# Merging the mixers of a two-layer backbone: rows transposed and routed before their norm is known, and where the last layer's first expert weights are split

## The chip, the cores and the metric

One core of one Trainium2 chip. The metric is the device time of one launch in microseconds (us); the median of three runs of the kernel before is 2865.58 us. The engines are named as the profile names them: PE multiplies matrices (PEld loads its weights), DVE is the vector engine, ACT the scalar engine, POOL GpSimd; SP issues most transfers.

## What is computed

Two layers of a backbone over 1024 latent tokens of 1024 features and 256 context tokens (layer 0 alone carries the context on). Each layer mixes tokens in four groups, merges them into the stream with one projection, and sends the stream through 16 experts that each choose their tokens. The part that matters here, from the reference:

```python
def _modulate(x, g, shift, scale):
    return _rmsnorm(x, g) * (1 + scale) + shift
...
xl = xl + gt1 * mix_l
xl = xl + gt2 * _ec_moe(_modulate(xl, norm2_g[i], sh2, sc2), router_w[i], ...)
...
def _ec_moe(h, router_w, w_gate, w_up, w_down):
    aff = softmax((h @ router_w).astype(float32), axis=-1)
    cap = max(1, EC_CAPACITY_FACTOR * N // N_EXPERTS)
    gates, idx = top_k(swapaxes(aff, 1, 2), cap)
    xs = h[idx]
```

With r a row's reciprocal norm, a2 = g (1 + scale) and b2 = shift, a row that the experts see is h = r (x a2) + b2, and its 16 logits are r ((x a2) W) + b2 W. Each expert takes the 128 tokens of largest probability.

## The kernel before, in words

A layer runs in stages: norm, projections, the mixers (a software pipeline over heads), `merge`, `moe`. In `merge` PE multiplies the mixers' outputs with the output projection, a tile of 128 tokens at a time, in two halves m of 512 columns. Both factors are in two parts of 12 bits, so a product takes three matmuls (`mm3`), and a half is 8 steps k of three: 24 matmuls into the PSUM tile `mixp`. Layer 0 has ten tiles (eight of tokens, two of context), layer 1 eight.

Everything else of the stage is put between these matmuls by hand. `Line` is a list of generators; after each step k `line.tick()` runs what is due, and a `yield n` puts the next piece n ticks later. Inside `manual_schedule` PE, DVE and ACT execute in the order in which the program records, so the ticks set where a piece stands in each engine's queue. An engine whose next instruction waits holds up everything behind it. The generators are:

- `residual` (L1274 to L1334), one for each half: the products times the gate (L1281), the residual added (L1282), a sum of squares on ACT. After the second half come the reciprocal norm (`rstd_steps`, with a power on POOL and four corrections on DVE), the norm and the modulation in two halves (L1306 on DVE, L1308 on POOL, on DVE for the last pair), the row's way to DRAM (`hrow`), and two groups of four transposes (`h2p`) with their copies into `h2T`.
- `router`, after each second tile, for two tiles: 8 matmuls on four column groups of PE (`lg`), a copy (`lpart`), 2 matmuls that add the groups (`lgs`), and a softmax on DVE and ACT. POOL splits the probabilities for the later gathers (`take`).
- `prep`, for each pair of tiles: the four groups' norms, transposes (`cTp`) and two parts of the left factors of the next pair (L1228 on ACT, L1230 on DVE).
- `vectors`: the modulation's vectors on all partitions (a2 is made at L1250); for the context once more.
- `best_four`, `best_six`, `best_all` and, in layer 0, `best_ctx`: lists of the largest probabilities, sorted and joined by chains of short DVE instructions (L1392 to L1430), then the slot of each token (`assign`, L1462 to L1493). `best_all` ends with `columns(0)`: DVE marks the slots of an expert (`hot`, L1507), PE turns them into row numbers (`tkp`), DVE writes these as integers (`tkii`, L1519).

`moe` starts with an indirect DMA that POOL issues: it gathers the first expert's rows from `hrow` into `xg` (L1552). PE transposes them (`pT`), ACT and DVE split them (`xs`), and the products with the experts' weights begin (`moeP`). The weights come as pages of 1 MB (`ewr`), of which every 128 rows are a step: ACT writes the upper part (`ewh`), DVE the lower one (`ewl`, L107). The first steps have their lower part made on POOL: 12 in layer 1, of which 8 stand ahead of the gather in POOL's queue and 4 behind it; 4 in layer 0, 1 ahead and 3 behind. While layer 0's merge ends, PE also multiplies the next layer's modulation (`ada_p`).

```python
AHEAD, BEHIND = (4, 12), (3, 4)
...
stream = weights()
ready = [next(stream) for _ in range(AHEAD[i] - BEHIND[i])]
xg0 = gather_tokens(self.first[0])
ready += [next(stream) for _ in range(BEHIND[i])]
```

Of the kernel before, what the change touches and what calls it, by code (L numbers as in the profile page):

```python
# [14 lines left out]
ALU = mybir.AluOpType  # L15
# [29 lines left out]
# rows of the small vectors, per layer  # L45
# [8 lines left out]
class Line:  # L54
    """work in steps beside a main stream; a step yields the number of ticks to the next one (1 without)"""
# [23 lines left out]
class Kernel:  # L79
# [48 lines left out]
    def rstd_steps(self, out, ss, n, width, pool=False):  # L128
        """out = 1 / sqrt(ss / width + eps), n columns; pool: without the scalar engine's tables"""
# [26 lines left out]
    def setup(self):  # L156
# [8 lines left out]
        # small vectors, one feature per partition  # L165
# [6 lines left out]
        # silu of the two conditioning vectors, padded to 32 columns  # L172
# [6 lines left out]
    def tables(self):  # L179
        """constants, side by side in one array"""  # L180
# [21 lines left out]
        # tokens of the same tile that come before  # L202
# [36 lines left out]
    def mod_feature(self, i, m):  # L239
        """the first norm's scale and shift, one feature per partition: modA, modB [128, 2 (c, ctx), 8 k]"""  # L240
# [4 lines left out]
        # chunk j, slice s -> feature (4j + s) of 16: vector j // 2, k = 4 (j % 2) + s  # L245
# [9 lines left out]
    def mod_row(self, out, i, v, c):  # L255
        """vector v of the six of layer i on all partitions: out [128, 1024]"""
# [7 lines left out]
    def take_x(self, t):  # L264
        """a token tile of x; of the rows loaded before the last expert's output was there, with it added"""
# [15 lines left out]
    def normed(self, t0, n):  # L281
        """x * rstd of token tiles"""
# [12 lines left out]
    def normed_T(self, xn, k):  # L295
        """128 features of the tiles, transposed"""
# [5 lines left out]
    def norm1_start(self):  # L302
        """the first tiles without the modulation"""
# [11 lines left out]
    def norm1(self, i, side, start, then):  # L315
        """then: called after the first group of tiles"""
# [23 lines left out]
    def h(self, part, k, t0, n):  # L340
        """hT columns of n tokens from t0 (t0 >= 1024: context)"""
# [7 lines left out]
    def proj_latent(self, i):  # L349
        """token-major qc | kvc | kr (416 columns)"""  # L350
# [28 lines left out]
    def proj_va(self, i):  # L379
        """values of group A, token-major, [hi | lo] side by side: [128 tokens, 2 tiles, head, 2, 64]"""  # L380
# [27 lines left out]
    def proj_feat(self, i, c0, put, putc):  # L408
        """feature-major 256 columns from c0: put and putc (latent, context) take features 128 m .. and the first token"""
# [29 lines left out]
    def put_q(self, tiles, alloc):  # L439
        """queries of group A, scaled: head h as [hi; lo] on the halves of the partitions (odd heads [lo; hi])"""  # L440
# [10 lines left out]
    def put_k(self, tiles, alloc):  # L451
        """keys of group A: head h as [hi; hi] and [lo; lo]"""
# [15 lines left out]
    def pool_buf(self, n):  # L468
        """[128, n + 16] with zeros around the n tokens"""
# [18 lines left out]
    def pool_mix(self, w, us, n, out):  # L488
        """us: two pool_bufs of 128 features; out(t, p): takes the 256 outputs of token tile t"""
# [5 lines left out]
        for m, u in enumerate(us):  # L495
            # position 8 + t holds token t; window sums of the lower and the upper 64 features
# [28 lines left out]
    def fno_weights(self, i):  # L525
        """[cos part | sin part] of the channel transform times fno_w: [128, 2 k, 512]"""
# [37 lines left out]
        # fold t with N - t: cosine sums see X[t] + X[N - t], sine sums X[t] - X[N - t]  # L564
# [56 lines left out]
    def fourier_ctx(self, i, fl, out):  # L621
        """fl [128, 2, 256]"""
# [28 lines left out]
    def untranspose(self, cT, n, out):  # L651
        """two of [128, n * 128] feature-major to token-major"""
# [11 lines left out]
    def pt_steps(self, hi, lo, P, nchunk):  # L664
        """transposes of P [128 q, nchunk * 128] into hi, lo: [128 keys, chunk, 128 q] views"""
# [1383 lines left out]
```

## Time and profile before

| | |
|---|---|
| three runs | 2858.80, 2865.58, 2865.62 us; median 2865.58 |
| the profiled execution's own time: its span, first to last instruction | 2861.3 us, 4.3 below the median |
| PE, share of the span | 94% |
| DVE, ACT, POOL | 73%, 60%, 14% |
| merge of layer 0, first to last `mixp` | 593.8 to 733.2 us |
| from there to the first expert product | to 777.66 us |
| merge of layer 1 | 2084.7 to 2193.2 us |
| from there to the first expert products without a gap | to 2256.96 us |

No time outside the span is recorded for the profiled execution, so the span stands for its time. The page divides time by engine, by source line and into 40 slices; the chain of waits goes back from the last instruction to what released each one. A row of the timeline has the start, the duration, the engine, the line, the operation with output and inputs, and in brackets how long the engine was idle and who ended that. Rows of the same kind in a row are put together (x3), and their duration is that of all of them. Rows of matmuls overlap, so the cost of one is the distance between starts.

### The profile page before, as it was taken

The numbers are of one execution on the slowest core, as the hardware profiler recorded it, in microseconds if no ns is written. First come the engines' busy times: TensorE is split into PE (matmuls) and PEld (weight loads), VectorE is DVE, ScalarE is ACT, GpSimd is POOL, SyncE is SP. The second block draws the span as 40 slices with busy tenths as digits, with TensorE's granted clock in tenths as the row PEclk, the third lists the DMA queues.
The fourth block names the chain that finished last, engine by engine and source line by source line (L and its number), as shares of the span: only waits on it lengthen the run. The fifth ranks groups of instructions, "written<-read, shape, count | busy, mean of one in ns | idle before, by whom it ended". The sixth has DMA issues, their size and how long they took to land. (4 is left out here: it accounts for less than half of the span.)

```text
span 2861.3 us, 46062 instructions
## 1 busy us (share of the span) xinstructions
PE 2688.6 (94%) x16912; PEld 2130.0 (74%) x16912; DVE 2096.3 (73%) x4289; ACT 1704.0 (60%) x3272; POOL 401.1 (14%) x436
## 2 busy tenths in 40 slices
PE   7999899999699999999999999999997599999996
PEld 5788788887377677677676788888885488888874
DVE  5624687867877777777766842687868899899997
ACT  5422687964255555555544631598953477777774
POOL 0000120222301010101100000120223311000112
PEclk9999999999799999999999999999998799999998
DMA  7642301145578787887778554201154699999996
GB/s 302 216 140 63 92 22 49 56 160 206 215 283 293 271 295 276 281 283 284 282 281 292 162 200 135 60 24 56 57 184 152 245 360 380 359 387 387 383 385 224
DMA packets 228106, 628.22 MB, mean 220 GB/s; under 512 B 32390, under 2 KB 87302, under 8 KB 227880
## 3 DMA queue, kind: packets, MB, share of 16 engines
q1 hardware_dynamic: 206088, 578.54, 55.2%
q0 software_dynamic: 21648, 46.67, 6.5%
q8 instruction: 134, 2.20, 0.3%
q14 instruction: 92, 0.75, 0.1%
q10 hardware_dynamic: 144, 0.07, 0.0%
HBM read 564.20 MB, written 61.01 MB: 219 GB/s over the span
## 5 line engine op out<-in xcount | busy, mean ns | idle before, releaser
L106 ACT ACTIVATE ewh<-ewr 128x1024 fp32r<-128x1024 f32 x768 | 765.6, 1055 | 312.8 <-DMA ewr<-exp_w_down 97.6
L107 DVE TENSOR_TENSOR ewl<-ewr,ewh 128x1024 fp32r<-128x1024 f32 x752 | 873.5, 1217 | 74.6 <-ACT ewh L106 73.1
L113 PE MATMUL moeP<-ewh,xs 128*128 128x512 f32 x2048 | 670.1, 401 | 6.6 <-DVE xs L107 6.6
L113 PEld LDWEIGHTS moeP<-ewh,xs 128*128 128x128 f32 x2048 | 387.9, 190 | 107.1 <-issue 11.2
L113 PE MATMUL moeP<-ewl,xs 128*128 128x512 f32 x1024 | 407.1, 398 | 0.0
L113 PE MATMUL moeP<-ewh,ehs 128*128 128x512 f32 x1024 | 331.8, 397 | 1.7 <-ACT ewh L106 1.5
L113 PEld LDWEIGHTS moeP<-ewh,ehs 128*128 128x128 f32 x1024 | 192.2, 188 | 58.6 <-issue 12.3
L113 PEld LDWEIGHTS moeP<-ewl,xs 128*128 128x128 f32 x1024 | 194.5, 190 | 40.7
L113 PE MATMUL moeP<-ewl,ehs 128*128 128x512 f32 x512 | 201.7, 394 | 0.0
L113 PE MATMUL mixp<-woh,cT 128*128 128x512 f32 x576 | 201.6, 407 | 0.0
L1602 PE MATMUL cx<-ewr,cxo 128*32 128x256 f32 x3072 | 186.3, 382 | 0.0
L107 DVE TENSOR_TENSOR ptl<-pT,pth 128x512 fp32r<-128x512 f32 (+2 forms) x288 | 164.2, 580 | 19.4 <-ACT pth L106 18.4
L122 PE MATMUL pT<-ident,PA 128*128 128x128 f32 x928 | 145.7, 275 | 8.3 <-ACT oh L714 3.7
L1602 PEld LDWEIGHTS cx<-ewr,cxo 128*32 128x32 f32 x3072 | 90.1, 109 | 84.5 <-issue 34.6
L106 ACT ACTIVATE pth<-pT 128x512 fp32r<-128x512 f32 (+2 forms) x288 | 149.6, 536 | 4.3 <-PE pT L122 1.3
L1653 POOL DMA_INDIRECT xacc<-ey,tkii x31 | 49.3, 1589 | 703.4 <-PE cx L1602 472.7
L1103 DVE TENSOR_REDUCE mxA<-SD 128x1 f32<-128x512 f32 (+1 forms) x192 | 114.5, 597 | 38.5 <-PE SD L113 37.8
L122 PEld LDWEIGHTS pT<-ident,PA 128*128 128x128 f32 x928 | 112.5, 141 | 32.5 <-ACT oh L714 5.8
L113 PEld LDWEIGHTS mixp<-woh,cT 128*128 128x128 f32 x576 | 108.2, 188 | 25.3 <-issue 3.5
L113 PE MATMUL SD<-kT,qT 96*128 96x512 f32 x384 | 119.9, 420 | 5.7 <-ACT PA L1117 5.3
L113 PE MATMUL mixp<-wol,cT 128*128 128x512 f32 x288 | 113.3, 393 | 0.0
L1552 POOL DMA_INDIRECT xg<-hrow,tkii x32 | 57.0, 1782 | 400.5 <-ACT ehs L106 97.6
(413 smaller groups left out, 5266.4 us busy)
## 6 DMA issues: line engine op xcount, KB each, us to landing
ewr<-exp_w_gate SPq DMA_DIRECT2D x128, 1024.0 KB
ewr<-exp_w_up SPq DMA_DIRECT2D x128, 1024.0 KB
ewr<-exp_w_down SPq DMA_DIRECT2D x128, 1024.0 KB
ada_w<-ada_w SPq DMA_DIRECT2D x96, 512.0 KB
qkv<-qkvr SPq DMA_DIRECT2D x18, 512.0 KB
xacc<-xm SPq DMA_DIRECT2D x18, 512.0 KB
hrow<-xm SPq DMA_DIRECT2D x18, 512.0 KB
x<-xacc SPq DMA_DIRECT2D x18, 512.0 KB
```

The lines of the kernel that those rows point to most:

```text
L106: self.nc.scalar.activation(hi, src, AF.Copy)
L107: (lo_on or self.nc.vector).tensor_tensor(lo, src, f32(hi), ALU.subtract)
L113: self.nc.tensor.matmul(out, l, r, start=start, stop=stop)
L122: self.nc.tensor.transpose(out, src, self.ident[:p, :p])
L1103: nc.vector.tensor_reduce(mx[:, j:j + 1], u.S[j], axis=AX.X, op=ALU.max)
L1552: nc.gpsimd.indirect_dma_start(out=xg, out_offset=None, in_=self.hrow, in_offset=bass.IndirectOffsetOnAxis(ap=idl, axis=0))
L1602: nc.tensor.matmul(pc[32 * j:32 * j + 32, :], xc[:, kk % 2, kk // 2], r[:, j * 256:(j + 1) * 256], start=(kk == 0), stop=(kk == KT - 1), t ...
L1653: nc.gpsimd.indirect_dma_start(out=self.xacc, in_=y, in_offset=None, compute_op=ALU.add, out_offset=bass.IndirectOffsetOnAxis(ap=idl, axis=0))
```

## The change

In `residual` each half of x is multiplied by a2 at once (a new DVE instruction, L1288 of the new file), and its four transposes stand two ticks behind that; the copy follows a tick later. The row's norm is worked out beside it. `router` runs for each tile: 8 matmuls with the transposed rows as weights and the 16 router columns as the moving side (`lg`, no column groups and no second product), then one DVE instruction takes the norm's factor (negated) and the shift's logits, and the softmax follows with fewer instructions (the sum comes with the exponential). The rows for the gather are finished behind the router, both halves on DVE (L1315); POOL's additions are gone. `vectors` also loads b2 by feature (`b2c`) and multiplies it with the router's columns (8 matmuls `b2p` and a copy), three times in all.

In layer 1, `early` loads the first two pages of weights during the last tile and splits four steps on ACT and DVE (L1332); four more are held until the first gather's index is there (`issue_after`), and four follow the first transposes. No step of layer 1 is split on POOL. Layer 0 keeps its four.

```diff
-AHEAD, BEHIND = (4, 12), (3, 4)
+AHEAD, BEHIND = 4, 3
...
 def vectors(self, i, c):
...
+        col = self.small([128, KT], name="b2c")
+        nc.sync.dma_start(col, self.mods[i][c, 3 * D:4 * D].rearrange("(k p) -> p k", p=128))
...
+        yield 4
+        p = self.b1([128, 16], name="b2p")
+        for k in range(KT):
+            self.mm(p, col[:, k:k + 1].to_broadcast([128, 128]), self.rw[:, k], k == 0, k == KT - 1)
+        yield 2
+        nc.vector.tensor_copy(shift, p)
...
 def residual(t, p, m, ss, h2T):
...
             nc.vector.tensor_tensor(x[:, s], x[:, s], mg[:, s], ALU.add)
+            nc.vector.tensor_tensor(mg[:, s], x[:, s], a2[:, s], ALU.mult)
             yield 2
             self.sumsq(ss[:, m:m + 1], x[:, s], 512)
+            tp = self.b1([128, 4, 128], name="h2p")
+            for k in range(4):
+                self.tr(tp[:, k], mg[:, (4 * m + k) * 128:(4 * m + k + 1) * 128])
+            yield
+            q = slice((t % 2) * 128, (t % 2) * 128 + 128)
+            nc.scalar.activation(h2T[:, 4 * m:4 * m + 4, q], tp, AF.Copy)
             if m == 0:
                 return
...
+            p = self.b1([128, 16], name="lg")
+            for k in range(KT):
+                self.mm(p, h2T[:, k, q], self.rw[:, k], k == 0, k == KT - 1)
+            for _ in rs:
+                pass
+            nc.vector.tensor_scalar(rn, r2, -1.0, None, op0=ALU.mult)
+            yield
+            yield from self.router(p, rn, shift, t)
             for j in range(2):
                 s = slice(j * 512, (j + 1) * 512)
-                nc.vector.scalar_tensor_tensor(mg[:, s], x[:, s], r2, a2[:, s], op0=ALU.mult, op1=ALU.mult)
-                late = t >= 2 * n - 2
-                (nc.vector if late else nc.gpsimd).tensor_tensor(mg[:, s], mg[:, s], b2[:, s], ALU.add)
-                yield 2 if late or not j else 3
+                nc.vector.scalar_tensor_tensor(mg[:, s], mg[:, s], r2, b2[:, s], op0=ALU.mult, op1=ALU.add)
+                yield
             nc.sync.dma_start(self.hrow[row, :], mg)
-            turn(0)
...
+        def early():
+            self.raws, self.ready = self.matrices(i), []
+            raws = list(itertools.islice(self.raws, 4))
+            yield 7
+            for raw in raws:
+                hi, lo = [self.half([128, 1024], F32R, name=nm) for nm in ("ewh", "ewl")]
+                nc.scalar.activation(hi, raw, AF.Copy)
+                self.ready.append((hi, lo, raw))
+            yield
+            for hi, lo, raw in self.ready:
+                nc.vector.tensor_tensor(lo, raw, f32(hi), ALU.subtract)
+                yield
...
 def router(self, p, rn, shift, t):
+        nc.vector.scalar_tensor_tensor(lg, p, rn, shift, op0=ALU.mult, op1=ALU.subtract)
+        nc.vector.tensor_reduce(mx, lg, axis=AX.X, op=ALU.min)
         yield
+        nc.scalar.activation(e, lg, AF.Exp, bias=mx, scale=-1.0, accum_out=sm)
         yield
+        nc.vector.reciprocal(sm, sm)
+        nc.vector.tensor_scalar(aff, e, sm, None, op0=ALU.mult)
...
 def moe(self, i, with_ctx):
+        else:
+            stream, ready = self.weights(self.raws), self.ready
+            xg0 = gather_tokens(self.first[0])
+            with self.tc.issue_after(self.first[2].ins):
+                ready += itertools.islice(stream, KT - len(ready))
...
             prep_x(cur)
+            ready += itertools.islice(stream, KT // 2)
```

Three places show what this does to the queues. On PE, at the end of layer 1's merge (`tkh` and `afT` belong to the lists), there stood before:

```order
L113 MATMUL mixp<-woh,cT 128x512
L113 MATMUL tkh<-tkv,ident 32x64
L122 MATMUL h2p<-ident,xm 128x128 x4
L113 MATMUL tkh<-tkm,ident 16x128
L122 MATMUL h2p<-ident,xm 128x128 x4
L1352 MATMUL lg<-h2T,rw 32x256 x8
L113 MATMUL lgs<-tables,lpart 128x16 x2
```

and now:

```order
L113 MATMUL mixp<-woh,cT 128x512
L113 MATMUL tkh<-tkm,ident 16x128
L113 MATMUL mixp<-woh,cT 128x512
L113 MATMUL mixp<-wol,cT 128x512
L113 MATMUL mixp<-woh,cT 128x512
L122 MATMUL h2p<-ident,xm 128x128 x4
L113 MATMUL lg<-rw,h2T 128x16 x8
L1389 MATMUL afT<-ident,aff 32x64 x2
```

The last tile's first transposes are out of the tail, nine products behind their half, and each tile's `lg` has its own eight matmuls.

On DVE, from the slots of layer 1 to the first expert's split rows (`xs`), there stood before:

```order
L1493 TENSOR_TENSOR slot<-chv 128x128
L1507 TENSOR_TENSOR hot<-slot,tables 128x1024 x2
L1519 TENSOR_REDUCE tkii<-tkp 128x1
L1524 TENSOR_REDUCE tkg<-tkp 128x1
L1507 TENSOR_TENSOR hot<-slot,tables 128x1024
L1519 TENSOR_REDUCE tkii<-tkp 128x1
L1524 TENSOR_REDUCE tkg<-tkp 128x1
L1507 TENSOR_TENSOR hot<-slot,tables 128x1024 x3
L1519 TENSOR_REDUCE tkii<-tkp 128x1
L1524 TENSOR_REDUCE tkg<-tkp 128x1
L1507 TENSOR_TENSOR hot<-slot,tables 128x1024 x3
L107 TENSOR_TENSOR xs<-pT,xs 128x512 x2
```

and now:

```order
L1492 TENSOR_TENSOR slot<-chv 128x128
L1506 TENSOR_TENSOR hot<-slot,tables 128x1024 x2
L1518 TENSOR_REDUCE tkii<-tkp 128x1
L1523 TENSOR_REDUCE tkg<-tkp 128x1
L1506 TENSOR_TENSOR hot<-slot,tables 128x1024
L107 TENSOR_TENSOR ewl<-ewr,ewh 128x1024 x4
L1518 TENSOR_REDUCE tkii<-tkp 128x1
L1523 TENSOR_REDUCE tkg<-tkp 128x1
L1518 TENSOR_REDUCE tkii<-tkp 128x1
L1523 TENSOR_REDUCE tkg<-tkp 128x1
L1506 TENSOR_TENSOR hot<-slot,tables 128x1024
L107 TENSOR_TENSOR xs<-pT,xs 128x512 x2
```

Four lower parts of weights have come in behind the first index, for three of the `hot` rows that moved back.

On POOL, from the last norm's power to the gathers of layer 1, there stood before:

```order
L135 TENSOR_TENSOR rs_r<-rs_v,mhalf 128x1
L107 TENSOR_TENSOR ewl<-ewr,ewh 128x1024 x6
L1375 TENSOR_TENSOR lrest<-aff,take 128x32
L1376 CAST take<-lrest 128x32
L1377 TENSOR_TENSOR take<-lrest,take 128x32
L107 TENSOR_TENSOR ewl<-ewr,ewh 128x1024 x2
L1552 DMA xg<-hrow_16364,tkii 128x1024
L107 TENSOR_TENSOR ewl<-ewr,ewh 128x1024 x4
```

and now:

```order
L135 TENSOR_TENSOR rs_r<-rs_v,mhalf 128x1
L1374 TENSOR_TENSOR lrest<-aff,take 128x16
L1375 CAST take<-lrest 128x16
L1376 TENSOR_TENSOR take<-lrest,take 128x16
L1555 DMA xg<-hrow_16504,tkii 128x1024 x4
```

The twelve splits are gone from this queue.

## Rows read from the trace of the kernel before

**Rows 1.** The page: its first line.
```profile
span 2861.3 us, 46062 instructions
```

**Rows 2.** Windows: stretch, length, each engine's busy us (instructions), clock, DMA share, GB/s.
```profile
593.80:733.20 139.40, 137.61 (x729) 107.25 (x727) 100.48 (x341) 69.76 (x204) 37.43 (x41) 1.00 0.54 188
733.20:777.60 44.40, 18.75 (x139) 8.71 (x138) 35.82 (x103) 7.68 (x13) 18.57 (x10) 0.70 0.66 246
2084.70:2193.20 108.50, 108.39 (x573) 85.25 (x571) 71.41 (x227) 54.04 (x157) 28.68 (x31) 1.00 0.37 132
2193.20:2257.00 63.80, 14.97 (x92) 9.64 (x92) 58.23 (x152) 18.43 (x24) 36.28 (x18) 0.57 0.59 218
```

**Rows 3.** Windows: 20 us late in layer 1's merge.
```profile
2160.00:2180.00 20.00, 19.89 (x106) 14.86 (x105) 18.71 (x64) 4.27 (x12) 4.51 (x5) 1.00 0.20 80
```

**Rows 4.** Timeline of PE, layer 0's merge: start, us, engine, line, operation, count.
```profile
718.96 1.07 PE L1352 MATMUL lg<-h2T,rw 128*32 128x256 f32 x16
719.96 0.50 PE L113 MATMUL mixp<-woh,cT 128*128 128x512 f32 x1
722.13 0.51 PE L113 MATMUL lgs<-tables,lpart 128*128 128x16 f32 x4
722.50 0.48 PE L113 MATMUL mixp<-woh,cT 128*128 128x512 f32 x1
```

**Rows 5.** Groups by line, DVE, layer 1's merge: busy, mean ns, idle before.
```profile
L1281 DVE TENSOR_TENSOR xm<-mixp,gt 128x512 f32<-128x512 f32 x15 | 10.3, 685 | 6.2 <-PE mixp L113 6.0
```

**Rows 6.** Timeline of PE, then DVE, in layer 1's merge.
```profile
2103.05 0.39 PE L113 MATMUL mixp<-woh,cT 128*128 128x512 f32 x1
...
2106.87 0.69 DVE L1281 TENSOR_TENSOR xm<-mixp,gt 128x512 f32<-128x512 f32 x1
...
2110.46 0.69 DVE L1281 TENSOR_TENSOR xm<-mixp,gt 128x512 f32<-128x512 f32 x1 [0.80 <-PE mixp L113]
2111.18 0.69 DVE L1282 TENSOR_TENSOR xm<-xm 128x512 f32<-128x512 f32 x1
```

**Rows 7.** Timeline, layer 1 after the merge, in order of time.
```profile
2197.65 7.05 POOL L107 TENSOR_TENSOR ewl<-ewr,ewh 128x1024 fp32r<-128x1024 f32 x3
2197.72 2.30 DVE L142 TENSOR_TENSOR rs_t<-rs_r 128x1 f32<-128x1 f32 x1 [0.32 <-POOL rs_r L135]
...
2220.56 0.17 DVE L1371 TENSOR_TENSOR aff<-lex,lmx 128x32 f32<-128x32 f32 x1
...
2239.74 1.86 POOL L1552 DMA_INDIRECT xg<-hrow,tkii  x1 [13.04 <-DVE tkii L1519]
...
2245.05 1.94 PE L122 MATMUL pT<-ident,xg 128*128 128x128 f32 x8 [5.25 <-DMA xg<-hrow,tkii]
...
2248.63 7.67 DVE L1507 TENSOR_TENSOR hot<-slot,tables 128x1024 bf16<-128x1024 f32 x3
...
2256.96 0.79 PE L113 MATMUL moeP<-ewh,xs 128*128 128x512 f32 x1 [6.55 <-DVE xs L107]
```

**Rows 8.** The page, part 5: DVE's lower parts of the expert weights.
```profile
L107 DVE TENSOR_TENSOR ewl<-ewr,ewh 128x1024 fp32r<-128x1024 f32 x752 | 873.5, 1217 | 74.6 <-ACT ewh L106 73.1
```

**Rows 9.** Timeline, layer 0 after the merge.
```profile
749.52 0.19 DVE L1371 TENSOR_TENSOR aff<-lex,lmx 128x32 f32<-128x32 f32 x1
...
758.89 7.49 POOL L1552 DMA_INDIRECT xg<-hrow,tkii  x1 [5.15 <-DVE tkv L1397]
...
765.77 7.60 DVE L1471 TENSOR_SCALAR chd<-ident,chl 16x16 f32<-16x16 f32 x1
766.41 6.93 POOL L107 TENSOR_TENSOR ewl<-ewr,ewh 128x1024 fp32r<-128x1024 f32 x3
...
777.66 0.80 PE L113 MATMUL moeP<-ewh,xs 128*128 128x512 f32 x1
```

**Rows 10.** Timeline, the last expert's gather: DVE, then POOL.
```profile
2741.74 8.03 DVE L107 TENSOR_TENSOR ewl<-ewr,ewh 128x1024 fp32r<-128x1024 f32 x7
...
2743.12 7.51 POOL L1552 DMA_INDIRECT xg<-hrow,tkii  x1 [23.92 <-PE moeP L113]
```

More of the change, by code (lines that the diff above doesn't have):

```diff
@@ L1287, in residual @@
             nc.sync.dma_start(self.xacc[row, :], x)
[L1288 to L1289 removed]
+            s2, r2, rn = [self.small([128, 1], name=nm) for nm in ("ss2", "rs1", "rsn")]
             nc.vector.tensor_tensor(s2, ss[:, :1], ss[:, 1:], ALU.add)
[L1291 to L1298 removed]
@@ L1300, in put @@
[L1300 to L1302 removed]
+            rs = self.rstd_steps(r2, s2, 1, 1024, True)
+            next(rs)
+            yield
[5 more added lines that the diff above has]
+            nc.vector.tensor_scalar(rn, r2, -1.0, None, op0=ALU.mult)
@@ L1310, in residual @@
             nc.sync.dma_start(self.hrow[row, :], mg)
-            turn(0)
-            yield
-            put(0)
-            yield
-            turn(1)
-            yield
-            put(1)
-            yield
-            if t % 2:
-                yield from self.router(rw, h2T, t - 1)
+            if t % 2 and t // 2 in then:
+                yield from then[t // 2]()
+        def early():
[6 more added lines that the diff above has]
+                self.ready.append((hi, lo, raw))
+            yield
+            for hi, lo, raw in self.ready:
+                nc.vector.tensor_tensor(lo, raw, f32(hi), ALU.subtract)
@@ L1321, in residual @@
                 yield
-                if t // 2 in then:
-                    yield from then[t // 2]()
         n = 5 if with_ctx else 4
@@ L1339, in merge @@
                 for t in (2 * P, 2 * P + 1):
+                    if t == NT - 1 and not with_ctx:
+                        line.add(early(), 4)
                     mix(t, h2T)
@@ L1524, in columns, with matrices, weights @@
         nc.vector.tensor_reduce(g, p[:, 2:], axis=AX.X, op=ALU.add)
-        return ii, g
+        return ii, g, done
+    def matrices(self, i):
+        a = self.a
+        order = []
+        for e in range(NE + 1):
+            if e < NE:
+                order += [a["exp_w_gate"][i, e], a["exp_w_up"][i, e]]
+            if e:
+                order.append(a["exp_w_down"][i, e - 1])
+        for w in order:
+            for k2 in range(4):
+                raw = self.wpage([128, 2, 1024], name="ewr")
+                self.nc.sync.dma_start(raw, w[k2 * 256:(k2 + 1) * 256, :].rearrange("(k p) f -> p k f", p=128))
+                for kk in range(2):
+                    yield raw[:, kk]
+    def weights(self, raws, pool=0):
+        for n, raw in enumerate(raws):
+            hi, lo = [self.half([128, 1024], F32R, name=nm) for nm in ("ewh", "ewl")]
+            self.split(hi, lo, raw, lo_on=self.nc.gpsimd if n < pool else None)
+            yield hi, lo, raw
     def moe(self, i, with_ctx):
@@ L1529, in moe @@
         last = i == DEPTH - 1
-        def weights():
-            order = []
-            for e in range(NE + 1):
-                if e < NE:
-                    order += [a["exp_w_gate"][i, e], a["exp_w_up"][i, e]]
-                if e:
-                    order.append(a["exp_w_down"][i, e - 1])
-            for n, w in enumerate(order):
-                for k2 in range(4):
-                    raw = self.wpage([128, 2, 1024], name="ewr")
-                    nc.sync.dma_start(raw, w[k2 * 256:(k2 + 1) * 256, :].rearrange("(k p) f -> p k f", p=128))
-                    for kk in range(2):
-                        hi = self.half([128, 1024], F32R, name="ewh")
-                        lo = self.half([128, 1024], F32R, name="ewl")
-                        self.split(hi, lo, raw[:, kk], lo_on=nc.gpsimd if n * KT + 2 * k2 + kk < AHEAD[i] else None)
-                        yield hi, lo, raw[:, kk]
         def gather_tokens(idl):
@@ L1554, in gather_tokens @@
             return xg
-        stream = weights()
-        ready = [next(stream) for _ in range(AHEAD[i] - BEHIND[i])]
-        xg0 = gather_tokens(self.first[0])
-        ready += [next(stream) for _ in range(BEHIND[i])]
+        if with_ctx:
+            stream, ready = self.weights(self.matrices(i), AHEAD), []
+            ready += itertools.islice(stream, AHEAD - BEHIND)
+            xg0 = gather_tokens(self.first[0])
+            ready += itertools.islice(stream, BEHIND)
+        else:
+            stream, ready = self.weights(self.raws), self.ready
+            xg0 = gather_tokens(self.first[0])
+            with self.tc.issue_after(self.first[2].ins):
+                ready += itertools.islice(stream, KT - len(ready))
         takes = {}
@@ L1563, in take @@
             if e < NE:
-                takes[e] = (self.columns(e) if e else self.first), self.columns(e, True) if with_ctx else (None, None)
+                takes[e] = (self.columns(e) if e else self.first)[:2], self.columns(e, True)[:2] if with_ctx else (None, None)
         take(0)
```

58 lines of the change are left out of this document (15 added, 43 removed).

## The prediction

> **What bounds the kernel now.** I read the windows of the two stretches that the change touches first, then the groups by line inside them, then the timeline of their ends. The span is 2861.3 us [rows 1], and it stands for the execution's own time; the median of the runs is 4.3 above. In both merges PE is the bound: 137.61 of 139.40 us busy in layer 0 and 108.39 of 108.50 in layer 1, at the full clock [rows 2]. Any matmul added there is paid in full, and so is any wait put into PE's queue. Behind each merge PE has nearly nothing to do: 18.75 of 44.40 us and 14.97 of 63.80, at a mean clock of 0.70 and 0.57 [rows 2]. Those two tails are chains through DVE and POOL, and work taken out of them comes back in full. So the change has a price in the merges and a gain in the tails, and the question is which is larger.
>
> **PE's added matmuls.** A pair of tiles costs 719.96 - 718.96 = 1.00 us for `lg` and 722.50 - 722.13 = 0.37 for `lgs` [rows 4], 1.37 in all. The new `lg` is 8 matmuls a tile with 16 columns moving, the form of `lgs`, which has 4 records for 2 matmuls [rows 4]. So 8 cost 4 x 0.37 = 1.48 us; the old `lg` row, 8 matmuls in 1.00, bounds it below, and I let 0.3 above stand for unknown weight loads. Tiles whose router ends behind the last product belong to the tail. Layer 1: 7 tiles x 1.48 + 1.48 for `b2p` - 3 pairs x 1.37 = **+7.7 us**. Layer 0: 9 x 1.48 + 2 x 1.48 - 4 x 1.37 = **+10.8**. Together +18.5 (bounds about +9 and +24). The transposes keep their number.
>
> **PE's new waits.** Before, the transposes stood far behind the norm. Now they stand nine products behind their half: the order of PE's queue has that. Nine products take 722.13 - 719.96 = 2.17 us [rows 4] from start to start, and as the next product starts some 0.2 us before the last one's end, the place is about 1.9 us behind the half's end. When DVE is free, L1281 starts 0.04 us behind the last product (an estimate from the idle times that this product ends [rows 5, 6]), L1282 0.72 later [rows 6], and the new multiplication, at the same price, ends 0.04 + 3 x 0.72 = 2.2 us behind it. So PE waits some 0.28 us at every half, even at best: 15 halves of layer 1 and 19 of layer 0 give 4.2 and 5.3 us. That is the floor.
>
> DVE is often not free. One half's last product ended at 2103.05 + 0.39 = 2103.44, and its L1281 started at 2106.87, 3.4 us later [rows 6]. Only 5 of 15 such rows found DVE waiting for them (6.0 of 6.2 us of idle time there are theirs [rows 5]). The ten others of layer 1 come 0.4 to 3.7 us late, by the same subtraction, 20 us in sum; in layer 0 eleven of nineteen, 31 us in sum. Before, this cost PE nothing; now PE stands at the transposes until it is over. If all of it stayed, waits would be 24 and 37 us: the ceiling. Some goes: what made the row at 2106.87 late were the norm's two rows and the left factors' lower parts in front of it, and while PE waits, DVE catches up. Some comes: DVE, busy 18.71 of 20 us late in the merge [rows 3], gets the new multiplication, 0.7 a half, and a router for each tile, whose exponential it waits for in its queue. Walking the queues of the changed kernel half by half with these durations I come to about 13 us in layer 1 and 17 in layer 0. These I take, **+30 in sum**, between 9.5 and 61.
>
> POOL's additions go; they hide behind the products, so I count nothing for them. The three small loads on SP's queue (router columns, b2 by feature) stand ten ticks and more ahead of their use; if late, they would show as waits at `b2p`.
>
> **Layer 1's tail.** Before, POOL's splits meet DVE. Three of them from 2197.65 [rows 7] hold DVE's tiny norm corrections to 2.30 us and more, three rows of them (2.30, where the short row at 2220.56 takes 0.17), and three later list rows fare the same: some 13 us on the chain to the probabilities, which end 27.4 us behind the last product (2220.56 - 2193.2) [rows 2, 7]. Without them, and with the transposes ahead of the norm: DVE reaches the last half 1.1 us late because of the four weight rows of 1.2 us in front [rows 8], its three instructions with list rows between end at 3.4, transposes and copy at half clock at 5.2, `lg` at 7.2, the softmax at 9.5. So 18 us come back. From the probabilities to the gather it was 2239.74 - 2220.56 = 19.2 us [rows 7]; now more list rows stand between, about 1.1 us, so the gather starts at 9.5 + 20.3 = 29.8. From gather to transposes 5.3 (2245.05 - 2239.74) [rows 7]: 35.1. `hot` rows were stretched to 7.67 us for three by POOL's last splits [rows 7]; now DVE does one `hot` and four splits in the gather's shadow, about 6.1 us, and the split of the rows follows. 3.3 for transposes and splits and 2 for the half clock give products at 40.4. Before, they ran without a gap at 2256.96 - 2193.2 = 63.8 [rows 2, 7]; eight had been done ahead (1.8) and the rest began at half clock (1.4), so 63.4 counts. **Gain 23** (bounds 15, if DVE is late with the weight rows, and 25).
>
> The gather itself is the uncertain piece. With `hot` or `ewl` rows running on DVE one took 7.49 us [rows 9] and another 7.51 [rows 10]; the one in question took 1.86 [rows 7]. Now four `ewl` rows stand behind the first `hot`. I keep 1.86, as the row of the same place, and put the 5.6 us more into the range. The Trainium skill ("SBUF — State Buffer", Who interferes with whom) infers that such two-input additions and subtractions leave the making of descriptors alone, since it needs the other side of the shared port; by that rule the gather cannot become slow here, and the sum would not move. The two rows of 7.5 us speak against the inference.
>
> **Layer 0's tail.** Three POOL splits stay behind the gather. The probabilities end at 749.52, 16.3 us behind the last product, and the gather starts 9.4 later [rows 2, 9]. I expect the probabilities at 8.5, so the gather at 17.9. Then comes the gather, 1.86 to 7.49, three splits of 6.93 in all, and the context's slots held behind these: that row took 7.60 and ended with them at 773.4, 4.3 before the first product [rows 9]. 17.9 + 4.7 (the middle) + 6.9 + 4.3 = 33.8, against 777.66 - 733.2 = 44.5. **Gain 10.7** (bounds 4, and 17 if the context's chain gets ahead of the splits).
>
> **Sum.** +18.5 + 30 - 23 - 10.7 = +15. The execution would take 2876, the median 2865.6 + 15 = **2880 us**. The experts' stage keeps its products and loses four steps of lead in layer 1: eight are ready at the first product instead of twelve. I count nothing for it, as DVE makes the next ones at 1.2 us each [rows 8] while PE is at those eight; if that cover is gone, each step late costs PE up to 1.2 us.
>
> **The rivals.**
> 1. *The waits stay at their floor* and the tails win. For it: the late halves of before came from rows that move. Against it: DVE's share late in the merge. With floor waits: 18.5 + 9.5 - 33.7 = -6; with the tails' upper ends -14, **2852 to 2860**. Without any wait the change is worth 18.5 - 33.7 = -15, so it breaks even at 15 us of waits, and is faster by over 8.6 us (0.3%, about what a measurement here can tell from no change) below 7 us of waits, or below 15 with the tails' upper ends. Chance 0.27.
> 2. *In between*: waits of 10 to 24 us, **2862 to 2874**. Chance 0.25.
> 3. *The early weights come late.* The four L1332 rows stand ahead of the last half in DVE's queue and wait for two pages of 1 MB; if the pages get no buffer until the last tiles' rows free theirs, DVE stands there and the tail waits: at the tail's 218 GB/s [rows 2] two pages take 9.6 us (an estimate). 15 + 9.6 = +25, **2890**. For it, pages and rows share one pool; against, DMA is at 0.20 there [rows 3]. Chance 0.08.
> 4. *The gathers starve* behind `ewl` and `hot` rows: +5.6 in layer 1 and +2.8 in layer 0, **2889**. Chance 0.10.
>
> **How the numbers follow.** My forecast, waits of 24 us and more, has 0.30, and rivals 3 and 4, on the same side, 0.18: slower 0.48. Rival 2 is no change, 0.25; rival 1 faster, 0.27. The range, 2851 to 2899, reaches from rival 1 with good tails to waits of 40 us with one starved gather; the forecast's own is 2874 to 2892.
>
> **What would show it.** The merges' windows: from 139.4 and 108.5 us to some 167 and 129, with PE idle before `h2p` put down to DVE's `xm`, 17 and 13 us. If that idle time is under 5 in each, rival 1 holds. The tails: 63.8 to about 41 and 44.4 to about 34, with no DVE row of 2.3 us in layer 1. `lg` should be 16 records in about 1.5 us for a tile. Idle DVE time before L1332 put down to ACT or a DMA shows rival 3; a gather of over 4 us in layer 1, rival 4. A merge that grows by less than 30 us in both layers together proves me wrong.

## The result, and the profile after

The changed kernel takes 2891.07 us (median of 4 runs, 2888.35 to 2895.02), the kernel before 2862.86 (median of 4): a ratio of 1.0099, with a 95% interval of 1.0087 to 1.0112. It is 28 us slower. The forecast was slower, 2880 us, within 2851 to 2899; the side is right, the loss (15 us) was put at half of what it is.

The first line of the page of the changed kernel's profiled execution:

```profile
span 2888.8 us, 46427 instructions
```

Its windows, in the columns of [rows 2]: the merge of layer 0, from its end to the first expert product, and the same for layer 1.

```profile
593.70:769.10 175.40, 157.89 (x833) 125.46 (x831) 113.49 (x411) 73.81 (x220) 21.75 (x40) 0.98 0.47 167
769.10:802.70 33.60, 21.06 (x127) 10.38 (x126) 23.51 (x71) 6.32 (x11) 11.63 (x9) 0.70 0.63 232
2107.80:2245.20 137.40, 124.52 (x649) 99.07 (x647) 87.51 (x292) 60.75 (x174) 16.56 (x31) 0.98 0.37 134
2245.20:2281.10 35.90, 10.36 (x72) 8.80 (x72) 28.25 (x118) 6.39 (x12) 4.09 (x6) 0.52 0.52 186
```

Against [rows 2] the merges grew from 139.4 to 175.4 us and from 108.5 to 137.4, 65 us together. The tails fell from 44.4 to 33.6 and from 63.8 to 35.9. The difference of the spans is 27.5 us. Layer 1's merge starts at 2107.8 instead of 2084.7: of layer 0's 36 us, 13 had come back by then. From the end of layer 1's merge to the end of the program another 24.5 came back, of the 29 that this merge had added. (That tail is 27.9 us shorter, but before eight products had been done ahead of its last gap: from the ninth product on the gain is 24.)

Where the merges' time goes is in the groups of PE, layer 0's merge first, then layer 1's (columns as in [rows 5]):

```profile
L113 PE MATMUL lg<-rw,h2T 128*128 128x16 f32 x144 | 16.8, 258 | 0.0
L122 PE MATMUL h2p<-ident,xm 128*128 128x128 f32 x76 | 12.4, 287 | 17.5 <-DVE xm L1288 16.6 <-DVE rs_v L132 0.7 <-DVE tks L1392 0.2
...
L113 PE MATMUL lg<-rw,h2T 128*128 128x16 f32 x112 | 13.1, 258 | 0.0
L122 PE MATMUL h2p<-ident,xm 128*128 128x128 f32 x60 | 9.6, 283 | 12.9 <-DVE xm L1288 11.9 <-DVE rs_v L132 0.7 <-DVE tks L1392 0.2
```

The last numbers of a row are PE's idle time ahead of these instructions and what ended it. PE now stands 17.5 and 12.9 us before the transposes, and DVE's new row L1288 ends nearly all of it. Before, PE stood 1.8 and 0.1 us in these merges. One of the long waits, on PE's timeline in layer 1 (first half of the second tile):

```profile
2134.11 0.39 PE L113 MATMUL mixp<-woh,cT 128*128 128x512 f32 x1
2136.59 0.63 PE L122 MATMUL h2p<-ident,xm 128*128 128x128 f32 x4 [2.08 <-DVE xm L1288]
2136.97 0.48 PE L113 MATMUL mixp<-woh,cT 128*128 128x512 f32 x1
...
2138.21 0.63 PE L113 MATMUL mixp<-wol,cT 128*128 128x512 f32 x1
2138.64 1.05 PE L113 MATMUL mixp<-woh,cT 128*128 128x512 f32 x2
```

Behind the wait a product takes 0.43 us from start to start (2138.64 - 2138.21) instead of 0.23: the clock has fallen to half. The window of these 4 us has a granted clock of 0.57 (column seven):

```profile
2137.50:2141.50 4.00, 4.00 (x12) 3.13 (x11) 0.00 (x0) 0.34 (x1) 0.00 (x0) 0.57 0.13 51
```

And what DVE did ahead of that wait:

```profile
2128.98 0.23 DVE L1361 SCALAR_TENSOR_TENSOR lgn<-lg,rsn,b2r 128x16 f32<-128x16 f32 x1 [1.26 <-PE lg L113]
...
2131.07 0.88 DVE L1230 SCALAR_TENSOR_TENSOR cT<-cTp,vec,cT 128x256 fp32r<-128x256 f32 x2 [0.88 <-ACT cT L1228]
...
2132.20 0.74 DVE L1315 SCALAR_TENSOR_TENSOR xm<-xm,rs,b2v 128x512 f32<-128x512 f32 x1
2132.86 0.87 DVE L1230 SCALAR_TENSOR_TENSOR cT<-cTp,vec,cT 128x256 fp32r<-128x256 f32 x2
2133.65 0.74 DVE L1315 SCALAR_TENSOR_TENSOR xm<-xm,rs,b2v 128x512 f32<-128x512 f32 x1
2134.31 0.68 DVE L1286 TENSOR_TENSOR xm<-mixp,gt 128x512 f32<-128x512 f32 x1
2135.02 0.69 DVE L1287 TENSOR_TENSOR xm<-xm 128x512 f32<-128x512 f32 x1
2135.75 0.69 DVE L1288 TENSOR_TENSOR xm<-xm,a 128x512 f32<-128x512 f32 x1
```

DVE first waits for PE's logits (1.26 us), then for the left factors on ACT (0.88), then finishes the previous tile's rows (L1315 twice), and only then takes up the half for which PE waits.

The tails, in order of time, layer 0's (POOL and DVE) and layer 1's:

```profile
788.09 1.07 POOL L1555 DMA_INDIRECT xg<-hrow,tkii  x1 [5.32 <-PE afT L1389]
789.19 6.93 POOL L107 TENSOR_TENSOR ewl<-ewr,ewh 128x1024 fp32r<-128x1024 f32 x3
...
791.77 5.44 DVE L1506 TENSOR_TENSOR hot<-slot,tables 128x1024 bf16<-128x1024 f32 x1
797.14 0.22 DVE L1470 TENSOR_SCALAR chd<-ident,chl 16x16 f32<-16x16 f32 x1
...
2248.32 1.09 PE L122 MATMUL h2p<-ident,xm 128*128 128x128 f32 x4 [3.13 <-DVE xm L1288]
2249.20 3.43 PE L113 MATMUL lg<-rw,h2T 128*128 128x16 f32 x16
...
2254.34 0.22 DVE L1370 TENSOR_SCALAR aff<-lex,lsm 128x16 f32<-128x16 f32 x1
...
2273.57 1.86 POOL L1555 DMA_INDIRECT xg<-hrow,tkii  x1 [17.80 <-DVE tkii L1518]
2274.39 4.62 DVE L107 TENSOR_TENSOR ewl<-ewr,ewh 128x1024 fp32r<-128x1024 f32 x4
2279.05 1.94 PE L122 MATMUL pT<-ident,xg 128*128 128x128 f32 x8 [5.41 <-DMA xg<-hrow,tkii]
```

In layer 1 the last row of the probabilities starts 9.1 us behind the last product (2254.34 - 2245.2), where it was 27.4 [rows 7]; no DVE row is stretched. In layer 0 POOL's three splits still hold DVE: a `hot` row of 1.2 us takes 5.44, and the context's row (`chd`) stands behind it.

### The profile page after: what moved, and what is told of

Its sections match the earlier page's. It is cut to its first block, busy times and chain, and to the rows that moved or that the text cites. A ratio compares the mean times of both kernels' runs of the same rounds, so it can differ in the third digit from the quotient of the medians.

```text
span 2888.8 us, 46427 instructions
## 1 busy us (share of the span) xinstructions
PE 2722.8 (94%) x17068; PEld 2161.2 (75%) x17068; DVE 2097.7 (73%) x4377; ACT 1708.2 (59%) x3299; POOL 338.6 (12%) x421
## 4 chain that ended last, share of the span: by engine, by line
PE 64%; DVE 11%; DMA 6%; ACT 5%; issue 3%; POOL 1%; POOLq 0%; DVEq 0%; ACTq 0%
PE moeP L113 32%; PE cx L1612 5%; PE pT L122 4%; PE oA L113 3%; PE SD L113 3%; PE pF L113 3%; PE mixp L113 2%; DMA xgc<-hrow,tkii 2%; PE pD L113 2%; DMA xg<-hrow,tkii 1%; DVE ewl L107 1%; PE lg L113 1%; DMA xacc<-ey,tkii 1%; PE pV L113 1%; PE ada_p L223 1%
## 5 line engine op out<-in xcount | busy, mean ns | idle before, releaser
L113 PEld LDWEIGHTS moeP<-ewh,xs 128*128 128x128 f32 x2048 | 386.6, 189 | 101.2 <-issue 11.7
L106 ACT ACTIVATE pth<-pT 128x512 fp32r<-128x512 f32 (+2 forms) x288 | 150.1, 538 | 4.3 <-PE pT L122 1.3
L113 PEld LDWEIGHTS moeP<-ewl,ehs 128*128 128x128 f32 x512 | 96.2, 188 | 21.3 <-issue 0.4
```

What stands on the lines that cost most here:

```text
L113: self.nc.tensor.matmul(out, l, r, start=start, stop=stop)
```

## The experiments

All ran beside the kernel before. Idle times before `h2p` and stretches of the merges are those of each run's profiled execution; merges are given as layer 0 and layer 1.

**Transposes three ticks later.** In `residual`, for all but the last tile:

```diff
             self.sumsq(ss[:, m:m + 1], x[:, s], 512)
+            if t < 2 * n - 1:
+                yield 3
             tp = self.b1([128, 4, 128], name="h2p")
```

> The transposes of every half but the last tile's stand three ticks (nine products, about 2.1 us) later. Theory (PE's waits for DVE at the transposes, 28.5 us by the trace of the change, and the half clock behind some of them, about 10 us, make the loss; the tails keep their gain of 37 us): the idle time before h2p in the two merges falls under 5 us, no half clock in the merges, merges about 154 and 120 us, and the whole near 2891 - 28 - 9 = 2854 us, faster than the kernel before. Rival (the waits are only DVE's load seen from PE; later transposes make DVE or the router late instead, and the wait returns at another place): idle time in the merges stays over 15 us and the whole stays above 2870 us.

Measured: 2850.03 us, ratio to the kernel before 0.9958 (0.9941 to 0.9975). The windows:

```profile
593.60:746.30 152.70, 151.49 (x832) 124.55 (x831) 111.75 (x408) 72.25 (x220) 23.59 (x40) 1.00 0.51 181
746.30:777.50 31.20, 21.32 (x129) 10.18 (x128) 22.09 (x73) 6.32 (x11) 12.22 (x10) 0.79 0.84 305
2083.90:2203.30 119.40, 118.89 (x647) 97.77 (x645) 83.47 (x288) 57.88 (x171) 19.19 (x30) 1.00 0.40 146
2203.30:2241.40 38.10, 10.66 (x72) 8.85 (x73) 30.52 (x122) 8.19 (x15) 7.84 (x8) 0.56 0.57 203
```

PE is idle 1.2 and 0.5 us in the merges, the clock is full, and the tails keep their length within 2.4 us. So what the place in the queues cost is 41 us, and the change without it is 13 us faster than the kernel before. The waits did not come back elsewhere. The edit moves more than the transposes: all that follows them in the generator comes three ticks later too, and on DVE the previous tile's last two rows (L1315 of the change) now stand behind the next half's three rows instead of in front of them. What these two rows do by themselves is measured further down.

**One tick later** (the same edit with `yield 1`).

> The same by one tick (three products, 0.7 us). If a wait is simply the lateness of DVE at that place, each wait of the change shrinks by 0.7 us and the small ones vanish: the 28.5 us become about 14. If the half clock needs a wait of 2 us before it, it is gone from the merges: 2891 - 14 - 7 = about 2869 us. Rival (the half clock comes from the router's narrow products, which stay): it stays in the merges, about 2877 us.

Measured: 2864.56 us, ratio 1.0010 (1.0000 to 1.0020). The windows of the merges:

```profile
592.50:754.40 161.90, 153.49 (x832) 123.73 (x831) 112.98 (x409) 73.42 (x220) 19.21 (x40) 1.00 0.50 174
...
2089.30:2216.90 127.60, 120.27 (x648) 97.04 (x647) 86.26 (x293) 60.93 (x174) 14.71 (x31) 1.00 0.39 140
```

Idle times of 8.4 and 7.3 us, together 16, near the 14 of the subtraction, the longest wait before `h2p` 1.58 us. In part the sum meets by chance: the waits of 2.06 to 2.08 us fell by 1.1 and not by 0.7, as one of the two rows L1315 now stands behind the next half's rows. The merges fell to 161.9 and 127.6 us at a clock of 1.00, though the router's narrow products are all there. So these products by themselves did not bring the half clock here. In the change the half clock followed four of the seven waits of 2.06 us and more and none of the shorter ones. The whole is 4 us better than expected; layer 0's tail, 28.2 us instead of 33.6, has that much, and why is open.

**POOL's splits back.** Layer 1's first twelve steps as before the change, no `early`:

```diff
-                    if t == NT - 1 and not with_ctx:
-                        line.add(early(), 4)
...
+        ahead, behind = (AHEAD, BEHIND) if with_ctx else (12, 4)
+        stream, ready = self.weights(self.matrices(i), ahead), []
+        ready += itertools.islice(stream, ahead - behind)
+        xg0 = gather_tokens(self.first[0])
+        ready += itertools.islice(stream, behind)
```

> The change with layer 1's first twelve lower parts back on POOL, eight ahead of the gather and four behind it. Theory (layer 1's tail gains mostly because POOL's splits no longer hold DVE): merges as in the change (175 and 137 us), layer 1's tail from 39 us back to about 55 to 60, the whole 2891 + 13 to 20 = 2904 to 2911 us. Rival (the tail's gain comes from the transposes being ahead of the norm, and the splits fit beside it): under 2896 us.

Measured: 2909.62 us, ratio 1.0169 (1.0152 to 1.0186), 18.5 above the change. The place is only partly the expected one. On POOL and PE at the end of layer 1's merge (which ends at 2256.1), with the merge's window first:

```profile
2106.00:2256.10 150.10, 130.76 (x649) 103.62 (x646) 100.95 (x291) 64.75 (x178) 35.66 (x39) 0.92 0.39 138
...
2231.80 7.06 POOL L107 TENSOR_TENSOR ewl<-ewr,ewh 128x1024 fp32r<-128x1024 f32 x3
2244.23 9.68 POOL L107 TENSOR_TENSOR ewl<-ewr,ewh 128x1024 fp32r<-128x1024 f32 x4 [1.18 <-ACT ewh L106]
...
2254.13 0.58 PE L113 MATMUL tkh<-tkm,ident 32*16 32x128 f32 x2 [5.89 <-DVE tkm L1427]
```

The splits hold DVE's lists while the merge still runs, and PE stands 5.9 us for a list and 3.6 more at the transposes. That merge takes 150.1 us, 12.7 more than in the change. PE's idle time, 19.3 instead of 12.9, is half of that; the clock makes most of the rest: the granted clock is 0.50 for 13.7 us from 2229.1, while PE waits and behind it, and again from 2253.0, inside the long wait. Its tail, to products without a gap, 44.9 instead of 35.9. The expected tail of 55 us did not come, because the eight splits ahead of the gather now all fall into the merge.

**The weights' part alone**: the kernel before with `early`, `matrices`, `weights` and the new start of `moe`, the old `residual`, `router` and `vectors`.

> The kernel before with the weights' part of the change alone: four early lower parts on DVE in the last tile, four behind the first gather's index, none on POOL in layer 1; the old norm, transposes and router. Theory: layer 0 and both merges as before (139 and 108 us), PE has no wait there; layer 1's tail loses the stalls of DVE of about 13 us and the stretched slot rows of about 5, against five us of splits on DVE: 63 to about 50 us, the whole 2863 - 13 = 2850 us. Rival (the early splits only move DVE's delay): 2863 us within 4.

Measured: 2847.35 us, ratio 0.9937 (0.9915 to 0.9958). The stretches are 140.0, 43.6, 108.4 and 45.6 us: all as before but layer 1's tail, 63.8 to 45.6. DVE's norm corrections take 0.16 us there, while the four early rows stand between the last half's own:

```profile
2195.06 0.66 DVE L1281 TENSOR_TENSOR xm<-mixp,gt 128x512 f32<-128x512 f32 x1
2195.84 1.20 DVE L1336 TENSOR_TENSOR ewl<-ewr,ewh 128x1024 fp32r<-128x1024 f32 x1
...
2202.28 0.16 DVE L142 TENSOR_TENSOR rs_t<-rs_r 128x1 f32<-128x1 f32 x1 [0.33 <-POOL rs_r L135]
```

So of the change's two parts one is worth 15 us and the other, as it stood, cost 44. The run before this one has the two in the other order: without the weights' part the rest costs 47 us, and the weights' part on top of it is worth 18.5.

**The new order for the last pair alone.** The old code for all other tiles; in `residual`:

```diff
+            if t >= 2 * n - 2:
+                nc.vector.tensor_tensor(mg[:, s], x[:, s], a2[:, s], ALU.mult)
...
+                if t < 2 * n - 1:
+                    yield 3
...
+                return
```

> The new order for the last pair of tiles of each merge alone (the first tile's transposes three ticks later, the last tile's at once), all other tiles with the old norm, transposes and pair router; the weights' part as in the change. Theory (the merges pay for the per-tile router and for waits, the tails gain from both parts): merges of about 143 and 112 us, tails of about 32 and 37, the whole 2847 - 12 - 9 + 6 = about 2832 us, faster than every other version. Rival (the tail's gain needs the lists of the earlier tiles to be further ahead, which the old order does not give): tails of 38 us and more, the whole 2840 us or above.

Measured: 2847.10 us, ratio 0.9941 (0.9927 to 0.9955). Merges of 144.0 and 114.7, tails of 35.4 and 41.1 us. The rival held by the whole, though layer 0's tail is under its 38 us: the merges are nearly as short as hoped, but the tails keep 4 and 3 us more than with the new order in every tile. Layer 0's gather starts 26.4 us behind the last product, against 19.2 there: the lists of the earlier tiles, which the pair router feeds later, are still in the chain.

**The gather's rows later.** In the change, ahead of the two rows L1315:

```diff
             yield from self.router(p, rn, shift, t)
+            if t < 2 * n - 1:
+                yield 4
             for j in range(2):
```

> The change, with the two rows L1315 that finish a tile for the gather four ticks later, behind the next half's own three rows on DVE (not in the last tile). Theory (the longest waits, 2.1 to 2.7 us at the first half of every second tile, come from these two rows of 0.74 us in front of that half's first row): those waits shrink by about 1.4 us, seven or eight times, so idle time in the merges falls from 30.4 to about 20 us, the half clock in the merges goes, the whole is about 2891 - 10 - 8 = 2873 us. Rival (DVE is late by its whole load; rows put later delay the next half instead): idle time stays over 27 us and the whole above 2885 us.

Measured: 2871.28 us, ratio 1.0030 (1.0017 to 1.0042). Idle times of 8.5 and 8.5 us, 17 in sum. The waits of 2.06 to 2.08 us became 0.76 to 0.79 wherever they stood at layer 0's or layer 1's second and fourth tile, 1.3 us less, which is the two rows (0.66 each from start to start). The later ones, with lists in front, stay at up to 1.85. No half clock. So these rows made most of the longest waits, and moving them alone gives back 20 of the 41 us that the first run gave.

**The logits by pair.** Three ticks later as in the first run, L1315 ahead of the router, and for all pairs but the last the logits of two tiles as before the change (`lg` on four column groups, `lpart`, `lgs`), the norm's factor still taken by the logits:

```diff
+                if t % 2:
+                    p = self.b1([128, 256], name="lg")
...
+                        nc.tensor.matmul(p[g:g + 32], self.rw[:, k], h2T[:, k], start=(k < 4), stop=(k >= 4),
+                                         tile_position=(0, g))
```

> As the run with transposes three ticks later, and for all pairs but the last the logits again by pair on four column groups with the second product that adds the groups (of rows without their norm; the factor still goes to the logits). Theory (with the waits gone, what the merges still pay is the per-tile router, 1.72 us a tile against 1.37 a pair): four pairs in layer 0 and three in layer 1 save 2 x 1.72 - 1.37 = 2.07 us each, 14 us, so merges of about 144 and 113 us and the whole about 2850 - 14 = 2836 us, faster than every version so far. Rival (the later router makes the lists of the earlier tiles late, which then stand in the tails, as in the run with the new order for the last pair alone): merges shorter by as much, but tails longer by 7 us or more in sum, the whole 2843 us or above.

Measured: 2855.74 us, ratio 0.9979 (0.9970 to 0.9988), 6 us slower than with a router for each tile (by spans 3.5). The rival again: merges of 149.7 and 116.2 us, with 5.9 and 3.4 us of PE's idle time back, and tails of 37.3 and 43.2, 6.1 and 5.1 longer. The last probabilities start 11.7 and 14.9 us behind the last product instead of 8.6 and 11.4, and from there to the gather it takes longer too, 6.0 us in layer 0 and 1.4 in layer 1.

**Each tile's logits on column groups.** As the first run, with 32 columns of the router as weights and 128 columns moving, for all but the last tile:

```diff
+            if t < 2 * n - 1:
+                p = self.b1([128, 128], name="lg")
+                for k in range(KT):
+                    g = 32 * (k % 4)
+                    nc.tensor.matmul(p[g:g + 32], self.rw[:, k], h2T[:, k, q], start=(k < 4), stop=(k >= 4),
+                                     tile_position=(0, g))
...
+                p = self.b1([128, 16], name="lgs")
+                self.mm(p, part, self.rsel, True, True)
```

> As the run with transposes three ticks later, with the logits of each tile (all but the last) on four column groups of PE, 128 columns moving, and one second product that adds the groups: the router's columns are the weights, as before the change, but for one tile. Theory (the dear part of the new logits is the loading of 128 columns of weights for each of 8 products; with 32 columns it goes): 8 products in 0.7 to 1.0 us and the second one in 0.19 instead of 1.72 us, so 0.5 to 0.8 us less in each of 16 tiles, against a copy and two ticks on the chain: merges about 6 and 5 us shorter, tails the same, the whole about 2850 - 9 = 2841 us. Rival (as with the router by pair, its later probabilities return as waits and tails): 2850 us within 4.

Measured: 2845.31 us, ratio 0.9941 (0.9922 to 0.9959). The eight products, and the one that adds, on PE's timeline:

```profile
2131.24 0.64 PE L1311 MATMUL lg<-h2T,rw 128*32 128x128 f32 x16
2131.81 0.50 PE L113 MATMUL mixp<-woh,cT 128*128 128x512 f32 x1
...
2133.31 0.29 PE L113 MATMUL lgs<-tables,lpart 128*128 128x16 f32 x2
2133.45 0.48 PE L113 MATMUL mixp<-woh,cT 128*128 128x512 f32 x1
```

0.57 and 0.14 us, against 1.71 in the change; whether the 32 columns of weights or the four column groups make the difference, the run does not tell. The merges are 5.3 and 4.2 us shorter, the tails 1.0 and 1.9 longer, the whole 5 us faster than the first run: half of what the merges gave, and between the expected 2841 and the rival's 2846 to 2854.

**No split on POOL in layer 0.** As the first run, with layer 0's four steps behind the gather and on DVE:

```diff
-            stream, ready = self.weights(self.matrices(i), AHEAD), []
-            ready += itertools.islice(stream, AHEAD - BEHIND)
+            stream, ready = self.weights(self.matrices(i)), []
             xg0 = gather_tokens(self.first[0])
-            ready += itertools.islice(stream, BEHIND)
...
+            ready += itertools.islice(stream, AHEAD)
             prep_x(cur)
```

> As the run with transposes three ticks later, with layer 0's four first lower parts on DVE too, among the rows of the context's slots behind the first gather, and none on POOL. Theory (what holds layer 0's tail, 31 us, is POOL's three splits of 6.9 us, behind which DVE's row for the context's slots stands until they end): without them that row takes 0.2 us, four splits of 1.2 us come in, and the first product comes 3 to 6 us earlier: tail 25 to 28 us, the whole 2844 to 2847 us. Rival (the tail hangs on the gather's transfer or the modulation's loads): tail 30 us or more, the whole unchanged or slower.

Measured: 2846.98 us, ratio 0.9939 (0.9922 to 0.9955). Layer 0's tail is 28.7 us, 2.5 shorter, where 3 to 6 had been expected. DVE's `hot` in it takes 1.23 us and four splits 1.2 each. The whole gains 3 us: the splits now stand in DVE's own queue. One more thing came up in layer 0's merge of this run: 3.4 us at half clock without a long wait, behind a list's products, 0.3 us of idle time and the sixteen narrow records of `b2p`:

```profile
697.21 2.03 PE L113 MATMUL b2p<-rw,b2c 128*128 128x16 f32 x16
699.08 1.10 PE L122 MATMUL h2p<-ident,xm 128*128 128x128 f32 x4
...
700.83 1.05 PE L113 MATMUL mixp<-woh,cT 128*128 128x512 f32 x2
```

So narrow products with a short wait can be followed by it too. They need not be: the run with transposes three ticks later has the same sequence, with the same 0.3 us, at full clock.

**Both.**

> The two runs before this together: transposes three ticks later, logits of each tile on four column groups, layer 0's first splits on DVE. Theory: the gains lie in different stretches, 5 us from the column groups and 3 us from the splits on 2850 us, so about 2842 us, the fastest of all versions. Rival: within 2 us of either alone (2845 to 2847 us), because layer 0's tail is then set by the later probabilities.

Measured: 2843.68 us, ratio 0.9940 (0.9926 to 0.9953), with merges of 147.4 and 115.3 and tails of 30.8 and 39.9. The two do not add up in full: it is 1.6 us below the better one, at the edge of the rival. Of the versions measured it has the lowest median, 17 us below the kernel before; the runs from 2843.7 to 2850.0 are not told apart by their intervals, so what is said of differences among them rests on their windows.

## Why the prediction was right on the side and short on the size

- **The tails** were sized well. Layer 1: probabilities at 9.5 us behind the last product, measured 9.1; the gather at 29.8, measured 28.4; gain 23, measured 24.5 by the time of everything behind the merge. Layer 0: 33.8 to the first product, measured 33.6; gain 10.7, measured 10.8 there and 13 by the start of layer 1's merge. In layer 0 that is luck in part, as three steps were off and cancelled: the gather started at 19.0 instead of 17.9, it took 1.07 instead of 4.7, and from the end of POOL's splits to the first product it was 6.6 us instead of 4.3. One more detail was off: what POOL's splits held was a `hot` row in front of the context's, not the context's own.
- **The waits** were sized well too: 17 and 13 us forecast, 17.5 and 12.9 measured (less 1.8 and 0.1 before). The walk of the queues that gave the forecast is not written out half by half, so only its sum can be compared. The trace has waits of 0.24 us where DVE is free, near the 0.28 of the floor:

```profile
2143.96 0.39 PE L113 MATMUL mixp<-woh,cT 128*128 128x512 f32 x1
2144.59 0.63 PE L122 MATMUL h2p<-ident,xm 128*128 128x128 f32 x4 [0.24 <-DVE xm L1288]
```

  and some of 2 us where the previous tile's last two rows stand in front. The runs with one and three ticks and with the later rows show this cause from both sides.
- **The term that was mis-sized is PE's added work**, +18.5 forecast. The new logits take 1.71 us a tile, not 1.48:

```profile
2127.08 1.86 PE L113 MATMUL lg<-rw,h2T 128*128 128x16 f32 x16
2128.79 0.47 PE L113 MATMUL mixp<-woh,cT 128*128 128x512 f32 x1
```

  By the distances between starts `lg` and `b2p` add 13.3 and 9.6 us where I had 10.8 and 7.7: 4.4 us more in sum.
- **A term was missing: what a wait does to the products around it.** The products themselves take 4.9 us more in each merge (116.9 to 121.8 and 92.8 to 97.7 us, by distances, PE's idle time left out). Each merge has two stretches of 3.4 us with a granted clock of 0.50 (from 622.2 and 731.4, 2137.7 and 2171.8), in which seven or eight products lose 0.2 us each, about 3 us a merge. The rest is the last product ahead of a wait. It counts until its end, 0.39 us as in the rows at 2134.11 and 2143.96, while one with work right behind it takes 0.25 to the next start; 17 products of layer 0's merge have a wait behind them instead of 4, and 13 of layer 1's instead of 1. The text had priced waits at their own length, and the clock only in the tails. Four more transposes in each merge and slower small groups add 2.1 and 1.6 us. Logits 4.4, products 9.8 and small groups 3.7 too little, less 1.5 for the waits and 3.7 for the tails, which came out better than forecast: 12.7 us, the distance from the forecast's sum (14.8, rounded to 15) to the spans' 27.5.
- **The rivals.** Waits at their floor, the faster case, did not come; the run with three ticks, with 1.7 us of waits, comes nearer to the text's case without any wait, 15 us faster than the kernel before: it was 12.7. Late pages did not show: DVE has no idle time ahead of the four rows L1332. The starved gather did not either: the first gathers took 1.07 and 1.86 us, in layer 1 with a `hot` and four split rows on DVE right behind the index. Two later gathers of layer 1, among DVE's split rows, took 5.43 and 4.16 us, and PE waited 0.5 us at most for them. What made the gathers of [rows 9, 10] take 7.5 us stays open; no run was made for it.
- **Readings and sums that were off.** Of the 15 halves in layer 1's merge before, eight and not ten others came late, with the same 20 us in sum. Of the first three stretched rows on DVE two are norm corrections (2.30 us) and one is a list's row (2.41). The range's upper end adds up to 2896 and not 2899 by its own terms, and rival 2's lower one to 2860 and not 2862. None of this moves the forecast.

In numbers: +36.0 and +28.9 in the merges, -12.9 and -24.5 behind them, the 27.5 us between the spans.

## What to carry to other kernels

When a step is moved ahead in an engine's queue, count how long its producer's chain is from the same starting point, row by row: nine products were 1.9 us, three DVE rows 2.2, and that difference and the lateness of a busy DVE cost 41 us that three ticks of patience, for the transposes and all that follows them, gave back. Split a change into its parts before judging it: one half of this one was worth 15 us and hidden by the other. And a product made cheaper early in a chain can return as lists that come late at its end; the tail has to be read again each time.

## What was not expected of the hardware

A wait of PE of 2.06 to 2.73 us in the midst of an otherwise full merge was followed by 3.4 us at half clock (0.43 instead of 0.23 us a product) in four of seven cases of the change. In the run with POOL's splits back, whose merges have the same seven waits, it followed five of them, so it is not tied to one place. In the runs with one tick and with the later rows, whose waits reach 1.85 us, none was. The one stretch behind narrow products and 0.3 us of idle time, in the run without splits on POOL, leaves open what exactly brings it. Eight products with 128 columns of weights and 16 moving took 1.71 us; with 32 columns of weights and 128 moving, on four column groups, 0.57. And a product with a wait behind it cost PE 0.39 us instead of 0.25, beside the wait itself.
